# Row loads through six buffers, fewer stores of the indexer parts, and Relu in place in PSUM, in a hybrid attention block

## The chip, the cores and the metric

The kernel runs on one core of one Trainium2 chip. The core has a matrix engine (TensorE, PE in the profile; PEld is its weight load), a vector engine (VectorE, DVE), a scalar engine (ScalarE, ACT), a general engine (GpSimd, POOL) and SyncE (SP), whose queue issues all DMA transfers of this kernel but those of a rare repair path. The metric is the device time of one execution in microseconds (us).

## The reference

One layer over 2048 rows of width 1024, in float32, cut to what matters here:

```python
xn = rms_norm(h, norm_gain[layer])
proj = xn @ w_in[layer]
qa, ka, va, ga, qb, kb, vb, gb, iq, ik, iw, za, zb = jnp.split(proj, offsets, axis=-1)
...
ya = chunked_relpos_attention(qa, ka, va, rel_bias[layer]) * jax.nn.silu(ga)
...
# dsa_sparse_attention, for each block of 128 queries:
logits = jax.nn.relu(jnp.einsum('bqhd,bsd->bqhs', iqb, ik))      # 8 indexer heads of 32
score = jnp.einsum('bqhs,bqh->bqs', logits, iwb).astype(jnp.float32)
_, idx = lax.top_k(score, top_k)                                 # 256 keys per query
...
merged = gate_a * (ya @ w_branch_a[layer]) + gate_b * (yb @ w_branch_b[layer])
h = h + merged @ w_out[layer]
```

The change touches two places: the normalisation of x with the indexer's part of the projection (`iq`, `ik`, `iw`, and `kb`, which rides with them), and the scores (`logits`, `score`).

## The kernel before

**Precision.** PE multiplies a reduced form of float32, so every operand is split: `h` is the value rounded by a copy on ACT, `l` the rest, a subtraction on another engine. A product is three matmuls (`mm3`, L193 to 199): high by high, high by low, low by high.

**The start: indexer projections (L213 to L374).** The rows of x come in four groups of 512, in the order 2, 3, 0, 1. `load_x` (L235) brings a group transposed (k along partitions, eight k-tiles) into one of two tiles `x32`. `squares` (L253) brings the same rows untransposed in four tiles of 128 x 1024 (`xrow`, 512 KB each, tag `gt`, two buffers) and squares and sums them on ACT (L258). `root_columns` (L262) makes the reciprocal roots by Newton steps on DVE. `root_rows` (L269) spreads them on POOL, transposes them on PE (L273) and copies them on ACT (L274). The first two groups are split without the root (`split_u`, L245) and multiplied by it when the product is evacuated. The other two are multiplied first (`split_x`, L207): a multiply on DVE (L209), the copy on ACT (L210), and the subtraction (L211), of eight k-tiles two on DVE and six on POOL. `chain(i, m)` is the product of one group with one of three column tiles m, 24 matmuls of 512 columns in an accumulator; there are five accumulators. `evac_i` (L286) rotates (m = 0), splits into `eh` and `el`, and stores the parts.

The stores go to DRAM: `iqD` (indexer queries) and `kB` (keys of the sparse attention), and to SBUF `ikT` (indexer keys, four copies by partition). Each is a transfer of its own for the high and the low part and for each strip of rows: 16 for m = 0, 2 for m = 1 and 6 for m = 2, so 24 a group.

**The main projections (L1156 to L1182).** `steps` go over column units and groups; each accumulator takes 24 matmuls and is evacuated. After each, `tick` calls `pump(PUMP)`, which lets two generators go on until a budget of cost is used up. The costs are written by hand in the `yield`s.

**The search stage, beside the main projections.** `logits` (L418): for each block of 128 queries, in two halves of four heads and in pieces of up to 512 keys, one matmul per head into a PSUM tile `lg` (five in rotation), Relu on ACT into an SBUF tile `r` (four buffers, L438), and the weighted sum into `sc`: head 0 on DVE (L441), heads 2 and 6 on POOL (L443 and L444), the others on DVE (L446). `search` (L456) finds the threshold of the 256 largest scores of two blocks at a time by eight counting passes, on DVE and ACT, then marks the keys (L514 to L532). `norm_again` (L1146) splits groups 2 and 3 a second time during the main projections; there all subtractions are on POOL.

When both generators have ended and 138 ticks have passed, the attention starts beside the remaining projections (`tick`, L1131), and later runs alone with the branch products, the output product and the final norm.

The order of instructions on each engine and in SyncE's queue comes from the framework's scheduler, which places them by a modelled timeline and by their order in the program. On the chip each engine and each queue runs in that order and waits where an operand or a buffer is not ready.

Of the kernel before, what the change touches and what calls it, by code (L numbers as in the profile page):

```python
# [20 lines left out]
S = 2048  # L21
# [21 lines left out]
PUMP = 3550  # L43
# [8 lines left out]
POOLH = (2, 6)  # L52
# [40 lines left out]
def block_kernel(ctx: ExitStack, tc: tile.TileContext, io, dbg=None):  # L93
# [22 lines left out]
    iqD = scratch("iqD", [2, 32 * H, S])  # L116
    mskD = scratch("mskD", [NT, 128, S], BF16)
# [89 lines left out]
    def split_x(s, k, src, root, e):  # L207

        nc.vector.scalar_tensor_tensor(src, src, gcol[:, k:k + 1], root, op0=OP.mult, op1=OP.mult)  # L209
        nc.scalar.activation(xh[s][:, k], src, AF.Copy)  # L210
        e.tensor_tensor(xl[s][:, k], src, f32(xh[s][:, k]), op=OP.subtract)  # L211

    with ExitStack() as ph:  # L213
# [24 lines left out]
        def load_w(m, k):  # L238
            st = xp.tile([128, 2, 128], F32, name="wis", tag="wis", bufs=4)
# [12 lines left out]

        def squares(i):  # L253
            for j in range(4):
                t = 4 * order[i] + j
                xr = tk.tile([128, D], F32, name="xrow", tag="gt", bufs=2)
                nc.sync.dma_start(xr, x[t * 128:(t + 1) * 128, :])
# [28 lines left out]
        def evac_i(i, m):  # L286
# [17 lines left out]
            e = [xp.tile([128, 512], F32R, name="e" + t, tag="e" + t, bufs=3) for t in "hl"]  # L304
            nc.scalar.activation(e[0], src, AF.Copy)
            (nc.gpsimd if m and i < 2 else nc.vector).tensor_tensor(e[1], src, f32(e[0]), op=OP.subtract)
            for z in range(2):
                q, k_ = iqD[z][:, cols], kB[z][:, cols]
                for dst, r0, r1 in (((q[0:32], 0, 32), (q[192:224], 64, 96), (k_[0:8], 32, 40), (k_[8:16], 96, 104)),
                                    ((q[32:160], 0, 128),),  # L310
                                    ((q[160:192], 0, 32), (q[224:256], 32, 64), (k_[16:64], 64, 112)))[m]:
                    nc.sync.dma_start(dst, f32(e[z][r0:r1]))
                if m == 0:
                    for y in range(2):
                        p = 64 * z + 32 * y
                        nc.sync.dma_start(f32(ikT[p:p + 24, cols]), f32(e[z][40:64]))
                        nc.sync.dma_start(f32(ikT[p + 24:p + 32, cols]), f32(e[z][104:112]))
# [12 lines left out]
        for m in (1, 2):  # L330
            for k in range(0, KT, 2):
                load_w(m, k)
            load_x(0, 4 * m - 4, 4 * m, halves[1])
        split_u(0, halves[0])
        split_u(0, halves[1])
        for k in range(0, KT, 2):
            load_x(1, k, k + 2)
# [986 lines left out]
```

## Time and profile before

| | us |
|---|---|
| median of 3 runs | 2149.0 |
| lowest and highest | 2148.93 and 2151.43 |
| the profiled execution | 2150.69 |
| its span, first to last instruction | 2148.9 |
| first matmul of the main projections, from the span's start | 137.64 |
| last piece of the search (mask store of the last block) issued | 860.8 |

Rows of the profile name an engine, a line of the kernel, the operation, the tile written and the tiles read (`out<-in`), and a count. In the groups of instructions, the busy time in us and the mean in ns of one follow, then the time that the engine stood idle just before them and what ended it (`<-`). In a timeline the first two numbers are the start and the length in us. SPq is SyncE's queue: its rows are DMA issues, not transfers. `xw` and `x` are the two buffers of `x32`, `xa` is an accumulator of the start, `acc` one of the main projections. A busy PE is not PE at its peak, and some matmul records can be missing from a trace.

### The profile page before, as it was taken

The page shows a single profiled execution, that of the slowest core. Times are in us where ns is not written, and L with a number is a line of the kernel's source. Part 1 is how long each engine was busy: PE and PEld are TensorE (multiplying, and loading weights), DVE is VectorE, ACT ScalarE, POOL GpSimd, SP SyncE. Part 2 cuts the span into 40 slices and gives each one's busy share as a digit, 9 for nine tenths or more (in the row PEclk, how much of TensorE's full clock was granted, in tenths as well). Part 3 has the DMA queues.
Part 4 walks back from the last instruction along what each step waited for, and adds up shares of the span by engine and source line. Part 5 has one row for each costly group of instructions (what it writes and reads, how often), then busy time and mean ns, then how long its engine had stood idle before and what let it go on. Part 6 is the DMA issues. An engine that isn't in the chain of part 4 may idle for free.

```text
span 2148.9 us, 33487 instructions
## 1 busy us (share of the span) xinstructions
PE 2038.5 (95%) x10858; PEld 1724.1 (80%) x10858; DVE 1334.1 (62%) x3255; ACT 1200.6 (56%) x2376; POOL 911.5 (42%) x941
## 2 busy tenths in 40 slices
PE   6499999999999999999899999999999999999998
PEld 5377778778886888888797888888889889887786
DVE  3538889696968956001232677866886688875444
ACT  5326555546545554212443787976887688873221
POOL 2426455646346362212321556445444543443420
PEclk9699999999999999999999999999999999999999
DMA  8445343435353332222755966457345641145642
GB/s 288 148 123 182 105 139 129 159 118 198 130 188 135 137 111 103 100 94 96 238 157 185 262 192 205 142 183 237 118 145 173 211 151 61 45 134 185 203 155 88
DMA packets 237939, 330.60 MB, mean 154 GB/s; under 512 B 29888, under 2 KB 120384, under 8 KB 237632
## 3 DMA queue, kind: packets, MB, share of 16 engines
q1 hardware_dynamic: 237760, 328.43, 47.4%
q8 instruction: 86, 1.41, 0.3%
q14 instruction: 93, 0.76, 0.1%
HBM read 221.43 MB, written 105.87 MB: 152 GB/s over the span
## 4 chain that ended last, share of the span: by engine, by line
PE 38%; DMA 6%; ACT 3%; issue 2%; DVE 2%; POOL 2%; SPq 1%; DVEq 0%; ACTq 0%; POOLq 0%
PE d L198 6%; PE po L1221 6%; PE O L969 5%; PE s L944 5%; PE pt L961 4%; PE O L879 3%; PE acc L198 3%; PE pt L869 2%; PE s L834 2%; DMA wst<-wP 1%; DMA mf<-mD 1%; DMA dst<-wB 1%; DVE P L765 1%; DMA dst<-wA 1%; POOL dw L1007 1%
## 5 line engine op out<-in xcount | busy, mean ns | idle before, releaser
L198 PE MATMUL acc<-xh,wt 128*128 128x512 f32 x2304 | 739.7, 395 | 1.3 <-ACT wt L189 1.2
L198 PEld LDWEIGHTS acc<-xh,wt 128*128 128x128 f32 x2304 | 433.1, 188 | 100.6 <-ACT wt L189 1.6
L198 PE MATMUL acc<-xl,wt 128*128 128x512 f32 x1152 | 453.8, 394 | 0.0
L190 POOL TENSOR_TENSOR wt<-wst,wt 128x512 fp32r<-128x512 f32 (+1 forms) x172 | 207.9, 1225 | 350.3 <-ACT wt L189 326.2
L786 POOL TENSOR_TENSOR ptl<-pf,pth 128x512 fp32r<-128x512 f32 (+1 forms) x144 | 179.9, 1249 | 217.0 <-ACT pf L782 157.0
L198 PEld LDWEIGHTS acc<-xl,wt 128*128 128x128 f32 x1152 | 217.3, 189 | 48.9
L789 DVE TENSOR_TENSOR ptl<-pt,pth 128x512 fp32r<-128x512 f32 (+1 forms) x288 | 187.7, 660 | 49.7 <-ACT pth L788 48.6
L446 DVE SCALAR_TENSOR_TENSOR sc<-r,iw,sc 128x512 f32<-128x512 f32 (+2 forms) x190 | 177.0, 951 | 53.5 <-POOL sc L444 35.9
L438 ACT ACTIVATE r<-lg 128x512 f32<-128x512 f32 (+2 forms) x304 | 152.4, 547 | 82.5 <-DVE sc L446 40.1
L944 PE MATMUL s<-kBt,qsB 128*128 128x512 f32 (+3 forms) x640 | 188.7, 385 | 2.5 <-issue 2.2
L788 ACT ACTIVATE pth<-pt 128x512 fp32r<-128x512 f32 (+1 forms) x288 | 161.1, 579 | 27.5 <-PE pt L961 13.2
L961 PE MATMUL pt<-ident,P 128*128 128x128 f32 x1088 | 166.9, 273 | 1.5 <-DVE ptl L789 0.5
L947 ACT ACTIVATE P<-P,mx 128x128 f32<-128x128 f32 (+15 forms) x128 | 154.6, 1208 | 18.5 <-DVE mx L765 17.8
L969 PE MATMUL O<-pth,vBt 128*128 128x256 f32 x544 | 148.2, 290 | 2.1 <-DVE yb L979 1.5
L969 PE MATMUL O<-ptl,vBt 128*128 128x256 f32 x544 | 147.2, 296 | 1.4 <-POOL ptl L786 1.0
L765 DVE CUSTOM_DVE_ANT_0 P<-s,mk,mx 128x512 f32<-128x512 f32 (+2 forms) x192 | 125.1, 652 | 35.2 <-PE s L944 29.3
L189 ACT ACTIVATE wt<-wst 128x512 fp32r<-128x512 f32 (+1 forms) x172 | 92.8, 577 | 87.2 <-DMA wst<-wP 83.6
L961 PEld LDWEIGHTS pt<-ident,P 128*128 128x128 f32 x1088 | 128.4, 140 | 10.5 <-ACT pf L782 1.6
L1007 POOL TENSOR_TENSOR dw<-dst,dw 128x512 fp32r<-128x512 f32 x64 | 82.8, 1293 | 114.0 <-ACT dw L1006 109.6
L494 ACT ACTIVATE jk<-sc,st 128x640 int8<-128x640 f32 (+6 forms) x49 | 71.3, 1455 | 82.3 <-DVE st L512 68.8
L436 PE MATMUL lg<-ikT,iqT 128*128 128x512 f32 (+2 forms) x304 | 98.3, 379 | 18.6 <-ACT r L438 18.6
L944 PEld LDWEIGHTS s<-kBt,qsB 128*128 128x128 f32 x640 | 103.8, 192 | 14.9 <-DVE mx L765 5.2
(233 smaller groups left out, 4234.2 us busy)
## 6 DMA issues: line engine op xcount, KB each, us to landing
wst<-wP SPq DMA_DIRECT2D x132, 256.0 KB
qs<-qA SPq DMA_DIRECT2D x128, 128.0 KB
kk<-kA SPq DMA_DIRECT2D x56, 256.0 KB
vs<-vA SPq DMA_DIRECT2D x56, 256.0 KB
bias<-biasD SPq DMA_DIRECT2D x32, 320.0 KB
xrow<-x SPq DMA_DIRECT2D x16, 512.0 KB
sBD<-ef SPq DMA_DIRECT2D x32, 256.0 KB
sAD<-ef SPq DMA_DIRECT2D x32, 256.0 KB
```

The costliest lines, as they stand in the source:

```text
L190: nc.gpsimd.tensor_tensor(wt[:, 1, k:k + n, c * 128:(c + 1) * 128], st, f32(hi), op=OP.subtract)
L198: nc.tensor.matmul(acc, a, b, start=(i == 0), stop=(i == n - 1))
L438: nc.scalar.activation(r[:, :w], lg[:, :w], AF.Relu)
L446: nc.vector.scalar_tensor_tensor(o_, r[:, :w], wv, o_, op0=OP.mult, op1=OP.add)
L765: nc.vector.tensor_tensor_reduce(dst, ps_, add, 1.0, FMAX if first else mx, OP.add, OP.min, accum_out=mx)
L786: nc.gpsimd.tensor_tensor(lo, pf, f32(hi), op=OP.subtract)
L788: nc.scalar.activation(hi, src, AF.Copy)
L789: nc.vector.tensor_tensor(lo, src, f32(hi), op=OP.subtract)
L944: nc.tensor.matmul(s_ps[:, :w], q[:, h, :], kBt[:, m, a:a + w], start=(m == 0), stop=(m == 1))
L947: nc.scalar.activation(P[:, e, :n], P[:, e, :n], AF.Exp, bias=mx[:, e:e + 1], scale=-1.0, accum_out=st["sum"][:, (u % 2) * 2 + e:(u % 2) * ...
L961: nc.tensor.transpose(pt[:, k, e, :], P[:, e, (kt + k) * 128:(kt + k + 1) * 128], ident)
L969: nc.tensor.matmul(o_, vBt[:, kt + k, :], src[:, k, :], start=(kt + k == 0 and n_ == 0), stop=(kt + k == b and n_ == 1), skip_group_check= ...
```

## The change

In the start:

- `load_rows` takes the row loads out of `squares`. Rows go in turn through three tags of two buffers each: `gt` and `iqT`, which are otherwise used later, and a new `xr`. The loads of group i stand earlier in the program: the first group's ahead of the second group's x, the second's ahead of the main loop, the third's and fourth's inside the first group's turn, with the third group's x between them. The fourth group's x is asked for in the second turn.
- `e` holds both parts in one tile, so one transfer stores both: 6 + 1 + 3 = 10 a group. The indexer keys go to a DRAM scratch `ikD` and from there into `ikT`, four transfers for two groups at a time.
- The subtractions of `evac_i` and `split_x` are all on DVE, those of `norm_again` too.
- The tile that weights pass through (`wis`) gets six buffers for four.

In the search stage:

- Relu writes back into the PSUM tile `lg`, and DVE reads it from there. All eight heads are on DVE; `r` is gone.
- The costs of the `yield`s and the budget `PUMP` (3850 for 3550) are new.

```diff
-PUMP = 3550
+PUMP = 3850
...
-POOLH = (2, 6)
...
+    ikD = scratch("ikD", [2, 32, S])
...
-    def split_x(s, k, src, root, e):
+    def split_x(s, k, src, root):
...
-        e.tensor_tensor(xl[s][:, k], src, f32(xh[s][:, k]), op=OP.subtract)
+        nc.vector.tensor_tensor(xl[s][:, k], src, f32(xh[s][:, k]), op=OP.subtract)
...
-            st = xp.tile([128, 2, 128], F32, name="wis", tag="wis", bufs=4)
+            st = xp.tile([128, 2, 128], F32, name="wis", tag="wis", bufs=6)
...
+        rows_ = {}
+
+        def load_rows(i):
+            for j in range(4):
+                n = rot("rows", 3)
+                t = 4 * order[i] + j
+                rows_[i, j] = (tk, tk, xp)[n].tile([128, D], F32, name="xrow", tag=("gt", "iqT", "xr")[n], bufs=2)
+                nc.sync.dma_start(rows_[i, j], x[t * 128:(t + 1) * 128, :])
+
         def squares(i):
             for j in range(4):
-                t = 4 * order[i] + j
-                xr = tk.tile([128, D], F32, name="xrow", tag="gt", bufs=2)
-                nc.sync.dma_start(xr, x[t * 128:(t + 1) * 128, :])
+                xr = rows_.pop((i, j))
                 nc.scalar.activation(xr, xr, AF.Square, accum_out=ss[:, 4 * i + j:4 * i + j + 1])
...
-            e = [xp.tile([128, 512], F32R, name="e" + t, tag="e" + t, bufs=3) for t in "hl"]
-            nc.scalar.activation(e[0], src, AF.Copy)
-            (nc.gpsimd if m and i < 2 else nc.vector).tensor_tensor(e[1], src, f32(e[0]), op=OP.subtract)
-            for z in range(2):
-                q, k_ = iqD[z][:, cols], kB[z][:, cols]
-                for dst, r0, r1 in (((q[0:32], 0, 32), (q[192:224], 64, 96), (k_[0:8], 32, 40), (k_[8:16], 96, 104)),
-                                    ((q[32:160], 0, 128),),
-                                    ((q[160:192], 0, 32), (q[224:256], 32, 64), (k_[16:64], 64, 112)))[m]:
-                    nc.sync.dma_start(dst, f32(e[z][r0:r1]))
-                if m == 0:
-                    for y in range(2):
-                        p = 64 * z + 32 * y
-                        nc.sync.dma_start(f32(ikT[p:p + 24, cols]), f32(e[z][40:64]))
-                        nc.sync.dma_start(f32(ikT[p + 24:p + 32, cols]), f32(e[z][104:112]))
+            e = xp.tile([128, 2, 512], F32R, name="e", tag="e", bufs=3)
+            nc.scalar.activation(e[:, 0], src, AF.Copy)
+            nc.vector.tensor_tensor(e[:, 1], src, f32(e[:, 0]), op=OP.subtract)
+            q, kb, ik = (t.rearrange("z r n -> r z n")[:, :, cols] for t in (iqD, kB, ikD))
+            for dst, r0, r1 in (((ik[0:24], 40, 64), (ik[24:32], 104, 112), (q[0:32], 0, 32), (q[192:224], 64, 96),
+                                 (kb[0:8], 32, 40), (kb[8:16], 96, 104)),
+                                ((q[32:160], 0, 128),),
+                                ((q[160:192], 0, 32), (q[224:256], 32, 64), (kb[16:64], 64, 112)))[m]:
+                nc.sync.dma_start(dst, f32(e[r0:r1]))
+            if m == 0 and i % 2:
+                half = slice(1024, 2048) if i == 1 else slice(0, 1024)
+                for a in range(4):
+                    nc.sync.dma_start(f32(ikT[32 * a:32 * a + 32, half]), ikD[a // 2][:, half])
...
+        load_rows(0)
+        for k in range(0, KT, 2):
+            load_x(1, k, k + 2)
         split_u(0, halves[0])
         split_u(0, halves[1])
-        for k in range(0, KT, 2):
-            load_x(1, k, k + 2)
         squares(0)
+        load_rows(1)
         for i in range(4):
             for m in range(3):
...
                     squares(1)
+                    load_rows(2)
+                    for k in range(0, KT, 2):
+                        load_x(2, k, k + 2)
+                    load_rows(3)
                 elif m == 0 and i < 3:
                     if i == 1:
                         squares(2)
                         squares(3)
                         root_columns(2, 2)
+                        for k in range(0, KT, 2):
+                            load_x(3, k, k + 2)
                     root_rows(i + 1)
                     for k in range(KT):
-                        split_x(SLOT[order[i + 1]], k, x32[(i + 1) % 2][:, k], roots_[order[i + 1]],
-                                nc.vector if k % 3 == 2 else nc.gpsimd)
+                        split_x(SLOT[order[i + 1]], k, x32[(i + 1) % 2][:, k], roots_[order[i + 1]])
...
-            if i < 2:
-                for k in range(0, KT, 2):
-                    load_x(i + 2, k, k + 2)
...
-                        r = tkl.tile([128, 512], F32, name="r", tag="r", bufs=4)
-                        nc.scalar.activation(r[:, :w], lg[:, :w], AF.Relu)
+                        lg = lg[:, :w]
+                        nc.scalar.activation(lg, lg, AF.Relu)
                         wv = iw[:, b, h:h + 1]
                         if h == 0:
-                            nc.vector.tensor_scalar(o_, r[:, :w], wv, 0.0, op0=OP.mult, op1=OP.add)
-                        elif h in POOLH:
-                            nc.gpsimd.tensor_scalar(r[:, :w], r[:, :w], wv, 0.0, op0=OP.mult, op1=OP.add)
-                            nc.gpsimd.tensor_tensor(o_, o_, r[:, :w], op=OP.add)
+                            nc.vector.tensor_scalar(o_, lg, wv, 0.0, op0=OP.mult, op1=OP.add)
                         else:
-                            nc.vector.scalar_tensor_tensor(o_, r[:, :w], wv, o_, op0=OP.mult, op1=OP.add)
-                        yield 0 if h in POOLH else 230 + w * (0.57 if h == 0 else 1.13)
+                            nc.vector.scalar_tensor_tensor(o_, lg, wv, o_, op0=OP.mult, op1=OP.add)
+                        yield 120 + w * 1.11
...
-            yield 2800
+            yield 3300
...
-                yield n[D] * 1.04 + 300
+                yield n[D] * 1.04 + 220
...
-                yield 2100
+                yield 2700
```

More of the change, by code (lines that the diff above doesn't have):

```diff
@@ L1151, in part @@
             for z in range(2):
-                split_x(SLOT[g], k + z, xs[:, z], roots[g], nc.gpsimd)
+                split_x(SLOT[g], k + z, xs[:, z], roots[g])
         return [lambda k=k: part(k) for k in range(0, KT, 2)]
```

## The prediction

> **What bounds the kernel now.** I read the page first, then busy time by stage, then the waits of TensorE (PE), then the timelines of the stage where PE is idle.
>
> ```profile
> span 2148.9 us, 33487 instructions
> PE 2038.5 (95%) x10858; PEld 1724.1 (80%) x10858; DVE 1334.1 (62%) x3255; ACT 1200.6 (56%) x2376; POOL 911.5 (42%) x941
> ```
> ```profile
> 0.00:38.80 38.80, 31.83 (x192) 29.06 (x192) 14.31 (x29) 19.56 (x41) 10.66 (x109) 1.00 0.92 331
> 38.80:137.60 98.80, 51.43 (x200) 39.66 (x200) 51.37 (x86) 37.35 (x69) 38.12 (x28) 0.74 0.44 136
> 137.60:900.00 762.40, 741.63 (x3356) 604.95 (x3355) 553.33 (x1188) 398.05 (x737) 365.00 (x332) 1.00 0.42 140
> 900.00:1150.00 250.00, 241.33 (x1262) 206.46 (x1261) 46.78 (x131) 83.26 (x205) 65.44 (x67) 0.99 0.45 145
> 1150.00:2149.00 999.00, 972.24 (x5855) 844.00 (x5853) 668.28 (x1822) 662.38 (x1326) 432.25 (x405) 0.99 0.52 162
> ```
>
> The second fence is busy time by stretch: length, then busy us (and instructions) of PE, its weight loads, DVE, ACT and POOL, granted clock, DMA share, GB/s. PE is the bound over the whole, and the change takes no matmul away. So only idle PE and PE at a lower clock can be won: 98.8 - 51.4 = 47.4 us idle in the start (indexer projections, to 137.6), at a mean granted clock of 0.74, and 762.4 - 741.6 = 20.8 us idle in the search stage (to about 900). The 35 us idle after 900 lie in code that the change does not touch.
>
> In the start, these are the waits of PE between 38 and 138 (us in total, times, longest), and the events around the third group:
>
> ```profile
> PE trr L273 <- POOL work L270: 24.8, 3, 17.3
> PE xa L198 <- DVE work L299: 10.4, 1, 10.4
> PE trw L323 <- DVE ea L300: 6.3, 1, 6.3
> PE xa L198 <- DVE xl L211: 5.6, 2, 4.6
> ```
> ```profile
> 42.37 0.17 DVE L264 TENSOR_SCALAR v<-ss 128x4 f32<-128x4 f32 x1 [18.68 <-ACT xrow L258]
> 85.63 1.06 ACT L258 ACTIVATE xrow<-xrow 128x1024 f32<-128x1024 f32 x1 [0.95 <-DMA xrow<-x]
> 86.81 0.17 DVE L264 TENSOR_SCALAR v<-ss 128x8 f32<-128x8 f32 x1 [13.94 <-ACT xrow L258]
> 93.24 1.22 PE L198 MATMUL xa<-xh,w 128*128 128x512 f32 x2 [0.21 <-ACT xh L210]
> 137.64 0.48 PE L198 MATMUL acc<-xh,wt 128*128 128x512 f32 x1
> ```
>
> All four go back to one thing. The roots of a group need the squares of its four row tiles (L258), and the squares wait for the rows' DMA. The third group's first matmul stands at 93.24, 7.6 us after the last square began at 85.63. Why the rows come late is in SyncE's queue:
>
> ```profile
> SPq L257 <- ACT xrow L258: 22.4, 9, 7.5
> ```
> ```profile
> 32.08 24.44 SPq L257 DMA_DIRECT2D xrow<-x  x9
> 59.55 1.84 SPq L312 DMA_DIRECT2D iqD<-eh  x2
> ...
> 73.26 0.43 SPq L312 DMA_DIRECT2D kB<-el  x1
> ...
> 80.82 0.35 SPq L257 DMA_DIRECT2D xrow<-x  x1
> ```
>
> Rows go through two buffers, so each load waits for a square (22.4 us of queue time). Then the 24 stores of the first group's parts hold the queue from 59.55 to 73.69, 14.1 us, and the second group's are mixed with the last row loads, which end at 80.82.
>
> **The start, part by part.** Row loads ahead, through six buffers: no instruction is added, the waits go. What is late next is the DMA rate.
>
> ```profile
> 20.00:30.00 10.00, 10.00 (x64) 9.01 (x63) 3.30 (x4) 4.68 (x9) 1.15 (x2) 1.00 1.04 401
> 0.00:10.00 10.00, 3.25 (x14) 3.20 (x15) 3.99 (x12) 5.75 (x13) 3.93 (x101) 1.00 0.65 198
> 140.00:150.00 10.00, 10.00 (x44) 8.07 (x43) 0.00 (x0) 1.65 (x3) 0.00 (x0) 1.00 0.42 121
> ```
> ```profile
> xrow<-x SPq DMA_DIRECT2D x16, 512.0 KB
> x<-xT SPq DMA_DIRECT2D x8, 512.0 KB
> xw<-xT SPq DMA_DIRECT2D x6, 512.0 KB
> wis<-wI SPq DMA_DIRECT2D x12, 128.0 KB
> xw<-xT SPq DMA_DIRECT2D x4, 256.0 KB
> ```
>
> These five add up to 17,920 KB or 18.35 MB. The first 10 us carry 1.98 MB (198 GB/s), the other 16.4 MB need 40.8 us at 401 GB/s: all has landed at 50.8. The last row lands earlier if it goes ahead of the fourth group's x (2.1 MB, 5.2 us: 45.6), later if tables of 1 MB go ahead of it (53.4). I take 50. Add the 7.6 us from last square to first matmul and 1.4 us for ACT and DVE, which now also evacuate the first two groups around then (before, 10.4 and 6.3 us of PE waits lay there; they go, as the first group's rows are now asked for ahead of the second group's x and its roots, begun at 42.37, come some 20 us earlier): third group at 59 instead of 93.24.
>
> From there to the main projections it took 44.4 us. Two groups of 72 matmuls at 10/44 = 0.227 us are 32.7 us. The subtraction of the split moves from POOL to DVE:
>
> ```profile
> L209 DVE SCALAR_TENSOR_TENSOR x<-x,gcol,work x8: 739/1768/1782, 101.8 to 111.6; 128x512 f32<-128x512 f32 x8
> L211 POOL TENSOR_TENSOR xl<-x,xh x6: 1711/1720/1745, 104.7 to 114.5; 128x512 fp32r<-128x512 f32 x6
> L211 DVE TENSOR_TENSOR xl<-xw,xh x2: 680/1214/1747, 101.2 to 113.3; 128x512 fp32r<-128x512 f32 x2
> ```
>
> The three figures are minimum, median and maximum in ns. With POOL subtracting beside it DVE's L209 takes 1768 at the median and 739 at best, so the two engines slow each other. Alone on DVE a step of the split is 0.74 + 0.68 = 1.42 us. Bounds: 8 steps are 11.4 us at these minima, 28 us at the medians' 3.5 us if the slow rows have another cause; I take the minima, since little is left on POOL there. The third group's first chain is then paced by DVE, 11.4 instead of 24 x 0.227 = 5.4 us, so +6.0; the fourth group's split (11.4) hides under the third's other two chains (10.9) but for 0.5; transposes and evacuation waits 1.3. Sum 32.7 + 6.0 + 0.5 + 1.3 = 40.5, so the main projections begin at 99.5, 38.1 us earlier. I take **37**. Bounds: 47 (row at 45.6, no slack) and 17 (16.6 us of slow split added, and a row 4 us later).
>
> Stores of the parts: 10 a group for 24, and four ikT loads a half from DRAM. An issue took 0.35 (80.82 row) to 0.92 us (59.55 row, two in 1.84): 3.5 to 9.2 us for 14.1. This lies beside PE work now, so I count nothing beyond the above; it costs up to 5 us if stores stand ahead of the last rows. The detour of ikT through DRAM adds a landing. The stores' rows show none of its length; PE's first logits matmul was at
>
> ```profile
> 158.36 1.03 PE L436 MATMUL lg<-ikT,iqT 128*128 128x384 f32 x5
> ```
>
> so 20.7 us of main projections cover it. Six weight buffers for four: nothing counted.
>
> **The search stage.** Relu in place, heads read from PSUM, no head on POOL.
>
> ```profile
> L446 DVE SCALAR_TENSOR_TENSOR sc<-r,iw,sc 128x512 f32<-128x512 f32 (+2 forms) x190 | 177.0, 951 | 53.5 <-POOL sc L444 35.9 <-ACT r L438 14.2
> L441 DVE TENSOR_SCALAR sc<-r,iw 128x512 f32<-128x512 f32 (+2 forms) x38 | 26.4, 694 | 36.8 <-ACT r L438 36.6 <-DMA iqT<-iqD 0.2
> L438 ACT ACTIVATE r<-lg 128x512 f32<-128x512 f32 (+2 forms) x304 | 152.4, 547 | 82.5 <-DVE sc L446 40.1 <-PE lg L436 19.5 <-POOL sc L444 14.6
> L674 DVE SCALAR_TENSOR_TENSOR el<-acc,eh 128x512 fp32r<-128x512 f32 x30 | 20.6, 686 | 21.9 <-ACT eh L673 20.8 <-DMA qB<-el 0.8 <-issue 0.3
> PE lg L436 <- ACT r L438: 18.6, 18, 2.8
> L446 DVE SCALAR_TENSOR_TENSOR sc<-r,iw,sc 128x512 f32<-128x512 f32 x125 | 127.2, 1034 | 30.9 <-POOL sc L444 20.8 <-ACT r L438 8.0
> ```
>
> DVE spends 177.0 + 26.4 = 203.4 us on six heads of eight and waits 35.9 more for POOL's sum. The same operation with one input in PSUM (L674) takes 686 ns at 512 columns, where L446 takes 1034. Scaled by that ratio, 304 heads cost 304 x 0.951 x 686/1034 = 192 us. Bounds: at L446's own 0.951 they cost 289 (86 more), at half of L674's 96 (107 less). I take 192, the nearest row being the same operation from PSUM to SBUF. So DVE does all eight heads in 11 us less than six. The later splits add 16 subtractions (16 x 0.68 = 10.9) and make the multiply beside them shorter. DVE's 553 us of 762 stay about 550: not the bound. Relu into PSUM has no row; L438's 547 ns and twice that are the ends, and ACT at 398 of 762 us covers even the second.
>
> Against it stands depth. A logits tile was free for PE once ACT had read it, with four more buffers of r behind; now it is free once DVE has read it, in order behind the search's long operations: five in flight for nine. PE's own waits there were 18.6 us in 18 places. Bounds: all 18.6 go; or each of the 18 gets longer by four heads of 0.69 us, +50. DVE's time per head, waits for POOL included, falls by a fifth ((203.4 + 35.9) to 192), and the new costs in the yields (120 + 1.11w, which at 512 gives 688, for L674's 686) spread heads better over the projections. I take **-6**. The thread costs add up to 510.9 thousand at 3850 a tick, 132.7 ticks, against 452.6 at 3550, 127.5; attention opens after tick 138 either way.
>
> [...]
>
> **Sum.** The profiled execution took 2150.7 us (span 2148.9 and 1.8 around it), 1.7 above the median of 2149.0. 2150.7 - 37 - 6 = **2108 us**, about 2.0% off. I call 0.2%, some 4 us, no change.
>
> **The rivals.**
> 1. *Start half won.* Stores of the first group's parts stand ahead of the last rows in SyncE's queue, or DVE does all sixteen L209 before the first subtraction, as it did eight before 101.2. The third group then starts near 75, gain 20: 2150.7 - 20 - 2 = 2129. For it: the queue did just that (73.26 and 80.82 rows). Chance 0.15.
> 2. *Better.* Row ahead of the last x, and PE's logits waits gone: -47 - 12 = 2092. Chance 0.11.
> 3. *Slower: the logits tiles.* PE stands at L436 for a tile that DVE has not read. It decides when the added wait passes the 37 us won in the start: 0.12 us for each of 304 heads. At the bound above, 18 waits longer by 2.8 us, it adds 50: 2150.7 - 37 + 50 = 2164. For it: five tiles, and one in-order DVE at 553/762 = 73%. Against: DVE gets less to do per head. Chance 0.08.
> 4. *PSUM heads dear.* If a head from PSUM costs DVE what L446 costs (0.951 us), DVE gets 86 us more than before in a stage with 209 idle. PE saw 18.6 us of the 203.4 us of heads before, 9%: 8 us, and the -6 is gone. 2150.7 - 37 + 8 = 2122. Chance 0.04. [...]
> 5. *It does not do what it says.* Squares still gate the loads (ACT is in order, and buffer seven waits for square one), so the rows land as late: 2149. Chance 0.04.
>
> **How the numbers follow.** Forecast (2097 to 2122) 0.58, rivals 0.15, 0.11, 0.08, 0.04, 0.04. The range 2090 to 2136 leaves out rivals 3 and 5 and the ends of 1 and 2. Faster: 0.58 + 0.15 + 0.11 + 0.04 = 0.88; same 0.04; slower 0.08.
>
> **What would show it.** Right: last row square before 55, third group's first matmul near 59, main projections near 100, clock near 1.0 in between; no SPq wait of L257 over some us; L446 near 690 ns; PE's lg waits under 18.6, now released by DVE. Wrong: squares past 70; L209 still near 1200 ns without POOL beside it; PE idle at L436 over 40 us.

## The result and the profile after

The changed kernel takes 2097.96 us (median of 4 runs, 2091.42 to 2099.17) against 2149.36 us of the kernel before on the same chip: a ratio of 0.9753, with a 95% interval of 0.9731 to 0.9774. That is 51 us less. 2108 was forecast, with a range of 2090 to 2136. The profiled execution took 2098.9 us.

Busy time by stretch follows, for the kernel after (columns as in the prediction). The stretches are counted from the first matmul of the main projections, at 108.23 us: the start ahead of it, its first 50 us, the next 150, the next 400, and what follows 858.23. The 150 us between the last two are left out; they hold 649 matmuls in both kernels.

```profile
38.80:108.23 69.43, 47.97 (x197) 37.79 (x197) 46.35 (x89) 30.10 (x60) 17.19 (x13) 0.83 0.57 200
108.23:158.23 50.00, 45.73 (x195) 37.22 (x194) 21.67 (x57) 23.38 (x52) 10.45 (x8) 0.93 0.64 207
158.23:308.23 150.00, 150.00 (x660) 122.37 (x659) 104.63 (x323) 81.85 (x165) 37.93 (x39) 1.00 0.38 127
308.23:708.23 400.00, 400.00 (x1909) 335.27 (x1909) 321.76 (x720) 225.03 (x410) 90.21 (x91) 1.00 0.45 153
858.23:2097.10 1238.87, 1202.45 (x7063) 1041.64 (x7061) 717.57 (x1952) 741.24 (x1524) 493.98 (x469) 0.99 0.51 159
```

The same stretches of the kernel before, counted from its first main matmul at 137.64:

```profile
137.64:187.64 50.00, 48.66 (x217) 39.27 (x216) 20.02 (x23) 21.91 (x49) 23.05 (x22) 1.00 0.64 201
187.64:337.64 150.00, 142.70 (x621) 114.65 (x620) 129.39 (x356) 85.34 (x173) 74.92 (x76) 1.00 0.39 129
337.64:737.64 400.00, 387.88 (x1820) 319.42 (x1819) 324.01 (x638) 217.69 (x399) 205.30 (x187) 0.99 0.44 149
887.64:2148.90 1261.26, 1225.93 (x7168) 1060.46 (x7166) 715.06 (x1952) 747.54 (x1533) 499.95 (x474) 0.99 0.50 158
```

Read the matmul counts, not only the busy time: in equal time they say how far PE has come. In the first 50 us of the main projections the changed kernel is 22 matmuls *behind* (195 for 217), in the next 150 us 39 ahead, in the next 400 us 89 ahead. Together that is 106, and at 0.2095 us each (400 / 1909) 22 us. The other 29.4 us are the earlier beginning of the main projections (137.64 to 108.23). 29.4 + 22 is nearly the whole difference of the spans, 51.8. After that nothing is won: PE is idle for 36.4 us of the last stretch, for 35.3 before. In the middle stretches before, PE was idle for 7.3 and 12.1 us and also a little slower while busy (0.2131 us a matmul for 0.2095 in the 400 us); after, it is never idle there.

The start in the timeline of the kernel after (start, length, then the instruction; PE, ACT, DVE and SyncE's queue SPq put together in order of time):

```profile
42.96 1.06 ACT L265 ACTIVATE xrow<-xrow 128x1024 f32<-128x1024 f32 x1 [1.25 <-DMA xrow<-x]
46.29 0.56 SPq L300 DMA_DIRECT2D cs<-csI  x1
46.95 0.54 SPq L260 DMA_DIRECT2D xrow<-x  x1
...
52.60 0.20 ACT L330 ACTIVATE iw<-trw 128x32 f32<-128x32 f32 x1 [2.71 <-PE trw L329]
52.70 1.05 ACT L265 ACTIVATE xrow<-xrow 128x1024 f32<-128x1024 f32 x1
...
57.89 1.04 ACT L265 ACTIVATE xrow<-xrow 128x1024 f32<-128x1024 f32 x1
60.10 0.17 DVE L271 TENSOR_SCALAR v<-ss 128x8 f32<-128x8 f32 x1
...
67.23 5.39 DVE L209 SCALAR_TENSOR_TENSOR xw<-xw,gcol,work 128x512 f32<-128x512 f32 x8 [2.61 <-ACT work L281]
68.70 1.65 PE L198 MATMUL xa<-xh,w 128*128 128x512 f32 x3 [0.22 <-ACT xh L210]
...
108.23 0.48 PE L198 MATMUL acc<-xh,wt 128*128 128x512 f32 x1
```

The last row load is issued at 46.95 and the third group's first matmul stands at 68.70, 21.8 us later. Between 44.0 and 52.7 ACT does no square: in its order copies stand ahead, those of the first group's evacuation and the small one of the indexer weights (L330), which waits 2.71 us for PE's transposes. Then six squares run back to back to 58.9. That does not make ACT the only limit. In this kernel the row loads whose landing the trace has took 6.3 to 10.6 us from issue to landing, which puts the last row at 53.3 to 57.6. Where the same load's landing is on record, in the kernel with the roots apart (below), it was issued at 46.90 and landed 9.7 us later, at 56.6 (the view of L260 from 46 to 48 us):

```profile
DMA to landing us min/median/max: 9.7/9.7/9.7
```

By that estimate the last square, begun at 57.89, came some 1.3 us after its row. The roots' small steps on DVE begin at 60.10 and end at 64.6; they stand between instructions of 0.7 us that evacuate the second group. All eight multiplies (L209) come before the first subtraction, 5.4 us during which PE has only the high parts.

PE's waits from 38 to 108 us, then those for logits tiles over the search stage:

```profile
PE xa L198 <- DVE work L306: 8.3, 1, 8.3
PE trw L329 <- DVE rs2y L134: 6.6, 1, 6.6
PE trr L280 <- POOL work L277: 4.1, 2, 3.3
PE xa L198 <- DVE xl L211: 2.9, 1, 2.9
...
PE lg L446 <- DVE sc L453: 3.8, 1, 3.8
PE lg L446 <- DMA ikT<-ikD: 0.5, 1, 0.5
```

Set beside the four waits that the prediction lists for the start: 24.8 us for the roots' rows (trr) became 4.1, and 5.6 for the low parts (xl) became 2.9. The other two stayed: 10.4 us for the evacuation (work) became 8.3, and 6.3 ahead of the weights' transposes (trw) became 6.6. 18.6 us of waits for logits tiles in 18 places became 4.3 in two. Groups of instructions of the kernel after:

```profile
L453 DVE SCALAR_TENSOR_TENSOR sc<-lg,iw,sc 128x512 f32<-128x512 f32 x175 | 129.8, 746 | 50.8 <-ACT lg L448 45.5
L448 ACT ACTIVATE lg<-lg 128x512 f32<-128x512 f32 x200 | 109.8, 577 | 39.1 <-PE lg L446 38.1
L209 DVE SCALAR_TENSOR_TENSOR x<-x,gcol,work 128x512 f32<-128x512 f32 x8 | 5.5, 739 | 0.0
```

A head of 512 columns takes 746 ns for 1034, and DVE now waits for ACT, not for GpSimd.

### The profile page after: what moved, and what is told of

The parts are those of the page before. It is cut to its first block, busy times and chain, and to the rows that moved or that the text cites. A ratio compares the mean times of both kernels' runs of the same rounds, so it can differ in the third digit from the quotient of the medians.

```text
span 2097.1 us, 33111 instructions
## 1 busy us (share of the span) xinstructions
PE 2027.5 (97%) x10858; PEld 1724.6 (82%) x10858; DVE 1309.3 (62%) x3363; ACT 1200.8 (57%) x2376; POOL 696.4 (33%) x757
## 4 chain that ended last, share of the span: by engine, by line
PE 41%; DMA 5%; ACT 2%; DVE 2%; issue 2%; SPq 1%; POOL 1%; DVEq 0%; ACTq 0%; POOLq 0%
PE po L1228 8%; PE d L198 8%; PE O L976 5%; PE s L951 5%; PE pt L968 5%; PE O L886 3%; PE acc L198 2%; PE s L841 2%; PE pt L876 2%; DMA vA<-eht 1%; DMA wst<-wP 1%; DMA dst<-wB 1%; DVE P L772 1%; DMA qs<-qA 1%; DMA dst<-wA 1%
## 5 line engine op out<-in xcount | busy, mean ns | idle before, releaser
L190 POOL TENSOR_TENSOR wt<-wst,wt 128x512 fp32r<-128x512 f32 (+1 forms) x172 | 206.2, 1215 | 604.5 <-ACT wt L189 590.0
L453 DVE SCALAR_TENSOR_TENSOR sc<-lg,iw,sc 128x512 f32<-128x512 f32 (+2 forms) x266 | 178.9, 680 | 90.4 <-ACT lg L448 82.2
L448 ACT ACTIVATE lg<-lg 128x512 f32<-128x512 f32 (+2 forms) x304 | 150.5, 525 | 53.9 <-PE lg L446 53.0
L846 ACT ACTIVATE P<-P,mx 128x640 f32<-128x640 f32 (+4 forms) x128 | 98.0, 767 | 23.7 <-DVE mx L772 23.2
L976 PEld LDWEIGHTS O<-pth,vBt 128*128 128x128 f32 x544 | 102.8, 189 | 10.5 <-ACT pth L795 2.5
```

What stands on the lines that cost most here:

```text
L190: nc.gpsimd.tensor_tensor(wt[:, 1, k:k + n, c * 128:(c + 1) * 128], st, f32(hi), op=OP.subtract)
L448: nc.scalar.activation(lg, lg, AF.Relu)
L453: nc.vector.scalar_tensor_tensor(o_, lg, wv, o_, op0=OP.mult, op1=OP.add)
L976: nc.tensor.matmul(o_, vBt[:, kt + k, :], src[:, k, :], start=(kt + k == 0 and n_ == 0), stop=(kt + k == b and n_ == 1), skip_group_check= ...
```

## The experiments

They ran in three groups on three chips; each ratio is against the kernel before on the same chip (medians 2150.73, 2149.25 and 2153.61 us). All kernels compute the whole layer.

**The start alone.** The kernel after, with the search stage, its costs and `norm_again` of before.

```diff
-PUMP = 3850
+PUMP = 3550
+POOLH = (2, 6)
...
-                        lg = lg[:, :w]
-                        nc.scalar.activation(lg, lg, AF.Relu)
+                        r = tkl.tile([128, 512], F32, name="r", tag="r", bufs=4)
+                        nc.scalar.activation(r[:, :w], lg[:, :w], AF.Relu)
...
+                        elif h in POOLH:
+                            nc.gpsimd.tensor_scalar(r[:, :w], r[:, :w], wv, 0.0, op0=OP.mult, op1=OP.add)
+                            nc.gpsimd.tensor_tensor(o_, o_, r[:, :w], op=OP.add)
...
```

> The kernel after with the search stage of before put back (Relu into r, heads 2 and 6 on GpSimd, the old costs and budget, the second splits' subtractions on GpSimd). After, the main projections began at 108.2 us for 137.6 before. Theory: the two halves of the change add up, so the start alone gives its 29.4 us: 2149.4 - 29 = 2120, main projections at 108 to 110, PE's wait for logits tiles still near 18.6 us. Rival: the earlier start is given back in the search stage, which was filled with DVE work: 2130 to 2145, logits waits over 25 us.

Measured: 2117.33 us, ratio 0.9849 (0.9829 to 0.9868), 33.4 us less. Main projections at 109.66. The logits waits are there nearly as before (14.8 us for 18.6), and in the first 50 us of the main projections this kernel does 202 matmuls, also fewer than the 217 of the kernel before:

```profile
PE lg L447 <- ACT r L449: 14.8, 17, 2.8
```
```profile
109.66:159.66 50.00, 45.80 (x202) 36.29 (x201) 25.00 (x61) 24.76 (x57) 21.47 (x20) 1.00 0.65 207
```

**The search alone.** The kernel before, with the search stage and the costs of after.

```diff
...
-POOLH = (2, 6)
...
-                        nc.scalar.activation(r[:, :w], lg[:, :w], AF.Relu)
+                        lg = lg[:, :w]
+                        nc.scalar.activation(lg, lg, AF.Relu)
...
-                        yield 0 if h in POOLH else 230 + w * (0.57 if h == 0 else 1.13)
+                        yield 120 + w * 1.11
...
```

> The kernel before with the search stage of after (Relu in place in PSUM, all heads on DVE, the new costs and budget); the start, and the second splits' subtractions on GpSimd, as before. Theory: the search part alone gives some 22 us (16 us of idle PE and 6 us of slower PE): 2127, PE's wait for logits tiles under 5 us, main projections still at 137.6. Rival: part of it came from the second splits on DVE or from the earlier start: 2133 to 2140, logits waits of 8 to 15 us.

Measured: 2124.56 us, ratio 0.9885 (0.9862 to 0.9908), 26.2 us less. Its waits for logits tiles, and its first 50 us from the first main matmul at 137.40 (in the next 150 and 400 us PE is never idle, with 660 and 1910 matmuls):

```profile
PE lg L435 <- DVE sc L440: 0.4, 1, 0.4
```
```profile
137.40:187.40 50.00, 48.37 (x217) 39.32 (x215) 16.96 (x30) 21.38 (x48) 11.76 (x10) 1.00 0.64 201
```

The two halves add to 59.6 us, together they give some 53 (2.47% of 2150.73). The intervals leave room for plain addition. In the first 50 us this kernel does 217 matmuls like the kernel before, the changed kernel 195; those 22 are about 5 us (50 / 217 = 0.23 us each). They do not show that the halves disturb each other: the start alone is 15 behind as well, so most of this loss comes with the new start and is already in its 33.4 us. The roots experiment below looks at what PE waits for there.

**Row loads alone.** The kernel before with `load_rows`, its six buffers and the new order of the loads; 24 stores and the split on GpSimd stay.

```diff
...
-                xr = tk.tile([128, D], F32, name="xrow", tag="gt", bufs=2)
-                nc.sync.dma_start(xr, x[t * 128:(t + 1) * 128, :])
+                xr = rows_.pop((i, j))
...
+        load_rows(0)
+        for k in range(0, KT, 2):
+            load_x(1, k, k + 2)
...
```

> The kernel before with only the row loads through six buffers and the new order of the loads of x; 24 stores a group, splits on GpSimd and search as before. Theory: the rows are most of the start's gain; without the other edits the third group's split is slowed by GpSimd beside it, so main projections at 112 to 118 and 2124 to 2130. Rival: the 24 stores hold SyncE's queue ahead of the last row loads, so the last square stands past 65 (58 after) and main projections at 122 or later, 2134 or more.

Measured: 2132.21 us, ratio 0.9919 (0.9900 to 0.9939), main projections at 120.40, last square at 56.07. The main projections begin later than the 112 to 118 that were expected. So the rows alone give 17 of the start's 29 us: they are early, but the split on two engines is slow, as its multiply shows (1500 ns at the mean here, 739 in the kernel after), and the 24 stores hold the start back too, as a run below shows for the kernel after (5 to 7 us):

```profile
L209 DVE SCALAR_TENSOR_TENSOR x<-x,gcol,work 128x512 f32<-128x512 f32 x8 | 11.5, 1500 | 0.0
```

**Two row buffers.** The kernel after, with all rows through `gt`'s two buffers.

```diff
-                n = rot("rows", 3)
+                n = rot("rows", 1)
```

> The kernel after with the rows through the two buffers of gt alone, the new order of loads kept. Theory: the six buffers let the rows come at the DMA's rate; with two, each load waits for a square, and the loads of x behind it in the queue wait too: third group at 75 to 85 for 68.7, main projections at 114 to 124, 2104 to 2114. Rival: the order of the loads and the fewer stores did it: third group at 68 to 72, time within 3 of after.

Measured: 2114.31 us, ratio 0.9820 (0.9804 to 0.9836); third group at 83.83, main projections at 123.31. SyncE's queue waits for squares again:

```profile
SPq L260 <- ACT xrow L265: 17.8, 10, 6.0
```

Against the kernel after beside it (2099.5) that is 14.8 us: six buffers are worth about that, and 13 us show in the start (123.31 for 110.19).

**24 stores a group.** The kernel after, with the stores of before (one a part and strip, `ikT` filled directly).

```diff
...
-                nc.sync.dma_start(dst, f32(e[r0:r1]))
+                    nc.sync.dma_start(dst, f32(e[z][r0:r1]))
+                if m == 0:
+                    for y in range(2):
+                        p = 64 * z + 32 * y
+                        nc.sync.dma_start(f32(ikT[p:p + 24, cols]), f32(e[z][40:64]))
...
```

> The kernel after with the 24 stores a group of before (two tiles e, ikT written from SBUF) put back. Rows alone had the main projections at 120.4 us, all start edits at 108.2 to 109.7. Theory: the stores issue beside PE work and come after the last row loads, so they are worth little: main projections at 108 to 112, time within 4 us of after. Rival: their 14 us of queue hold back the tables and the weights of the main projections, so they are most of the 11 us: main projections at 116 or later, 2105 or more.

Measured: 2102.09 us, ratio 0.9777 (0.9754 to 0.9800); third group at 73.14, main projections at 115.30. PE waits 8.6 us for the roots' rows where the kernel after waits 4.1:

```profile
PE trr L279 <- POOL work L276: 8.6, 2, 7.8
```

The start is 5 to 7 us later, past the 108 to 112 that were expected, but the intervals of the whole times overlap: a loss in the total is not shown.

**The split on GpSimd again.** The kernel after, with six of eight subtractions of the start's split on GpSimd.

```diff
...
-        nc.vector.tensor_tensor(xl[s][:, k], src, f32(xh[s][:, k]), op=OP.subtract)
+        e.tensor_tensor(xl[s][:, k], src, f32(xh[s][:, k]), op=OP.subtract)
...
+                                nc.vector if k % 3 == 2 else nc.gpsimd)
```

> The kernel after with six of eight subtractions of the start's third and fourth splits on GpSimd again (the second splits stay on DVE). Theory: GpSimd beside DVE slows both, L209 at 1250 to 1770 ns for 740, and this is most of the 11 us that rows alone lack: main projections at 115 to 119, time some 8 us above after. Rival: the split is off PE's path either way: main projections at 108 to 111, time that of after.

Measured: 2102.52 us, ratio 0.9788 (0.9765 to 0.9810); main projections at 113.67. The multiply by itself, with minimum, median and maximum in ns:

```profile
L209 DVE SCALAR_TENSOR_TENSOR xs<-xs,gcol,roots x16: 744/750/753, 132.1 to 619.1; 128x512 f32<-128x512 f32 x16
L209 DVE SCALAR_TENSOR_TENSOR x<-x,gcol,work x8: 740/1773/1785, 77.7 to 87.5; 128x512 f32<-128x512 f32 x8
```

In one kernel, the same operation takes 750 ns at the median where GpSimd has no part in the split and 1773 where it subtracts six k-tiles of eight. That settles why L209 was slow before (1768 at the median). The main projections begin 3.5 to 5.4 us later than in the two profiles of the kernel after (110.19 and 108.23), less than was expected (115 to 119). In the whole time a loss is not clear: the interval overlaps that of the first measurement of the kernel after (up to 0.9774), but not that of the second, below (up to 0.9763).

Rows (17.2 us), split (3.5 to 5.4) and stores (5 to 7) together come to 26 to 30 us, about the 29.4 of the start. The evacuation's subtractions on DVE and the six weight buffers were not tried by themselves.

**Relu into SBUF, no head on GpSimd.** The kernel after with the tile `r` again, four buffers; all heads on DVE.

```diff
-                        lg = lg[:, :w]
-                        nc.scalar.activation(lg, lg, AF.Relu)
+                        r = tkl.tile([128, 512], F32, name="r", tag="r", bufs=4)
+                        nc.scalar.activation(r[:, :w], lg[:, :w], AF.Relu)
+                        lg = r[:, :w]
```

> The kernel after with Relu into the four SBUF buffers r again; all eight heads on DVE, now from SBUF. Theory A: DVE's heads got cheaper because GpSimd no longer reads SBUF beside them; then a head of 512 takes some 740 ns here as well, PE's wait for logits tiles stays under 5 us, and the time is that of after, 2098 within 3. Theory B: the source in PSUM is what makes the head cheap; then a head of 512 takes 900 to 1030 ns, and the time is 2104 to 2115.

Measured: 2094.95 us, ratio 0.9753 (0.9726 to 0.9780), the same as the kernel after. So Relu in place is worth nothing that can be measured; that GpSimd takes no heads is what counts. The heads in three kernels (this one, the kernel after, and the start alone with two heads on GpSimd; minimum, median, maximum in ns):

```profile
L454 DVE SCALAR_TENSOR_TENSOR sc<-r,iw,sc x266: 465/746/1832, 117.9 to 779.5; 128x512 f32<-128x512 f32 x85, 128x384 f32<-128x384 f32 x24, 128x256 f32<-128x256 f32 x24
```
```profile
L453 DVE SCALAR_TENSOR_TENSOR sc<-lg,iw,sc x266: 457/742/754, 116.3 to 781.1; 128x512 f32<-128x512 f32 x84, 128x384 f32<-128x384 f32 x25, 128x256 f32<-128x256 f32 x24
```
```profile
L457 DVE SCALAR_TENSOR_TENSOR sc<-r,iw,sc x190: 471/748/1860, 117.6 to 775.0; 128x512 f32<-128x512 f32 x125, 128x384 f32<-128x384 f32 x35, 128x256 f32<-128x256 f32 x30
```

The medians agree; what differs is the tail. From PSUM no head takes more than 754 ns. From SBUF some take 1832, in this kernel few (mean 830 at 512 columns), with heads on GpSimd many (1025 in the start alone). This is the pattern of L209. Two heads of 512 columns show it, each begun while GpSimd subtracts for the weights' split (L190): the first of this kernel, the second of the kernel after.

```profile
735.32 1.30 POOL L190 TENSOR_TENSOR wt<-wst,wt 128x512 fp32r<-128x512 f32 x1
735.55 1.62 DVE L454 SCALAR_TENSOR_TENSOR sc<-r,iw,sc 128x512 f32<-128x512 f32 x1 [3.97 <-ACT r L448]
```
```profile
737.88 1.30 POOL L190 TENSOR_TENSOR wt<-wst,wt 128x512 fp32r<-128x512 f32 x1
738.37 0.75 DVE L453 SCALAR_TENSOR_TENSOR sc<-lg,iw,sc 128x512 f32<-128x512 f32 x1 [0.75 <-ACT lg L448]
```

With both inputs in SBUF the head ends at 737.17, 0.55 us after the subtraction's end at 736.62. Counted in the trace, all 28 heads over 1 us in this kernel end so, 0.54 to 0.55 us after such a subtraction at 512 columns (17 of them), 0.41 at 384 and 0.28 at 256. So the end of a slow head goes by the end of the subtraction, not by the head's own start. In the kernel after, 57 of the 266 heads run beside a subtraction on GpSimd and none is longer for it (754 ns at most). The head above is lengthened by less than GpSimd's whole 1.30 us (1.62 us for 0.75); 0.23 us of the subtraction had gone by when it began. Why the place of the input matters is not shown.

**The costs of before.** The kernel after, with the yields and the budget of before.

```diff
-PUMP = 3850
+PUMP = 3550
...
-                        yield 120 + w * 1.11
+                        yield 0 if h in (2, 6) else 230 + w * (0.57 if h == 0 else 1.13)
...
```

> The kernel after with the yields and the budget of before (3550 a tick, heads 2 and 6 at no cost). Theory: the cheaper heads did it, the costs only spread the work: PE's logits waits 4 to 10 us, time within 5 us of after. Rival: the new costs are what frees PE: waits of 15 us or more, 2108 or more.

Measured: 2095.87 us, ratio 0.9752 (0.9725 to 0.9779): the same. The costs are worth nothing that can be measured.

**Three logits tiles for five.** A test of the rival that the tiles run out.

```diff
-                        ln = rot("lg", 5)
+                        ln = rot("lg", 3)
```

> The kernel after with the logits in three PSUM tiles in rotation for five. Theory of the prediction's third rival: a tile is free only once DVE has read it, so fewer tiles let PE wait for DVE: 15 to 40 us of PE waits at the logits for 4.3, 2108 to 2130. Other theory: DVE has so much slack that three do: waits under 10, 2098 to 2104.

Measured: 2101.19 us, ratio 0.9759 (0.9743 to 0.9774), beside 2099.5 us of the kernel after on that chip, with overlapping intervals. The waits grow little:

```profile
PE lg L446 <- DVE sc L453: 3.8, 3, 3.4
```

Even three tiles are enough. Depth is not what bounds this stage.

**The roots apart.** The third group's roots waited in the kernel after for the squares of the fourth, since both are made in one pass over 8 columns (L271). Here each group has its own.

```diff
                         squares(2)
-                        squares(3)
-                        root_columns(2, 2)
+                        root_columns(2, 1)
...
+                    else:
+                        squares(3)
+                        root_columns(3, 1)
```

> The kernel after with the roots of the third and fourth group made apart (four Newton columns each), so that the third group does not wait for the fourth group's squares, which move behind the third group's first product in the program. After, the last six squares ran back to back from 52.7 to 58.8 though their rows had been asked for by 47, and the third group's first matmul came at 68.7. Theory: ACT's order, not the DMA, is what is late now, so the third group starts 4 to 8 us earlier, main projections at 101 to 105, time 2090 to 2094. Rival: the evacuation of the second group on DVE and PE's first two products end about then anyway: third group at 66 or later and the time of after.

Measured: 2091.2 us, ratio 0.9734 (0.9709 to 0.9759); the interval overlaps that of the kernel after (0.9731 to 0.9774), so a gain over it is not shown by this run. The third group begins 6.4 us earlier than in the kernel after, but the main projections at 109.23, no earlier:

```profile
62.27 1.22 PE L198 MATMUL xa<-xh,w 128*128 128x512 f32 x2 [2.40 <-ACT xh L210]
68.26 0.79 PE L198 MATMUL xa<-xh,w 128*128 128x512 f32 x1 [4.76 <-DVE work L306]
```

The expected earlier start did not come: much of the time won turned into a wait for the second group's evacuation. Nor was ACT's order the only thing late, as the theory had it: the last row landed at 56.6 here too. Yet the first 50 us of the main projections changed:

```profile
109.23:159.23 50.00, 50.00 (x226) 41.08 (x224) 23.60 (x66) 26.33 (x58) 10.20 (x8) 1.00 0.66 204
```

That is 31 matmuls more than the 195 of the kernel after, some 7 us (24 more than the 202 of its second profile, below). The order on DVE differs. First the kernel after (DVE and PE), then this one (DVE):

```profile
116.30 2.78 DVE L453 SCALAR_TENSOR_TENSOR sc<-lg,iw,sc 128x384 f32<-128x384 f32 x4
130.34 1.42 DVE L209 SCALAR_TENSOR_TENSOR xs<-xs,gcol,roots 128x512 f32<-128x512 f32 x2 [11.25 <-DMA wst<-wP]
131.67 0.61 DVE L453 SCALAR_TENSOR_TENSOR sc<-lg,iw,sc 128x384 f32<-128x384 f32 x1
...
132.33 0.69 PE L446 MATMUL lg<-ikT,iqT 128*128 128x384 f32 x1 [3.77 <-DVE sc L453]
```
```profile
124.79 0.62 DVE L455 SCALAR_TENSOR_TENSOR sc<-lg,iw,sc 128x384 f32<-128x384 f32 x1 [2.09 <-ACT lg L450]
129.58 1.42 DVE L209 SCALAR_TENSOR_TENSOR xs<-xs,gcol,roots 128x512 f32<-128x512 f32 x2 [4.18 <-DMA xs<-xT]
```

In the kernel after, the multiply of `norm_again` stands in DVE's order behind five heads (L451 and these four L453) and waits 11.25 us for a transfer: its operand is `xs`, though the profile names `wst` as the last to come. The heads behind it hold the logits tiles, and PE stands 3.77 us at L446. In this kernel six heads go ahead of the multiply, the sixth at 124.79, its tile is free in time, and PE has no wait for a logits tile in these 50 us. The granted clock is 1.00 there for 0.93. So the traces explain the wait by the order on DVE, and the wait with the lower clock makes up the difference in matmuls; no run changes this order alone. What else held the main projections at 109 us was not taken apart.

**The kernel after again, and the roots apart with later transposes.** Five rounds each on one chip; in the second, also the weights' transposes `weights_t` come one turn later.

```diff
...
-                    else:
-                        weights_t(i - 1)
+                    elif i > 1:
+                        weights_t(i - 2)
...
+        weights_t(2)
         weights_t(3)
```

> The kernel after once more, as it is, as the measure for the runs beside it: 2098 within 4. Its first profile had the main projections at 108.2 us.

> The kernel after with the roots of the third and fourth group made apart, and the transposes of the indexer weights (whose copy held ACT up until 53) one turn later. With the roots apart alone the third group started at 62.3 for 68.7, yet PE stood 12.6 us for L306, the evacuation of the first two groups, and the main projections began no earlier (109.2). Theory: without the copy ahead of them the squares end at 53 to 55, the third group starts at 57 to 60, and main projections at 103 to 106, 3 to 5 us under after in the same runs. Rival: the evacuations on DVE set the start, so main projections at 108 or later and the time of after within 2.

Measured: 2099.5 us, ratio 0.9750 (0.9737 to 0.9763), for the kernel after; 2092.7 us, ratio 0.9714 (0.9701 to 0.9727), for the other. These intervals do not overlap: it beats both kernels. Its third group begins at 62.11, not at 57 to 60, and its first main matmul stands at 109.86 for 110.19, so the expected gain in the start did not come here either. The first 50 us of main projections, the kernel after first:

```profile
110.19:160.19 50.00, 46.51 (x202) 37.40 (x201) 23.58 (x61) 24.14 (x55) 10.25 (x8) 0.97 0.66 205
```
```profile
109.86:159.86 50.00, 48.34 (x216) 39.08 (x215) 22.02 (x57) 24.57 (x54) 10.21 (x8) 1.00 0.64 205
```

14 matmuls more, some 3 us, and 0.3 us in the start; the profiled spans differ by 4.8 (2097.7 and 2092.9), the medians by 6.8. The rest of the gain has no place in these rows and stays open.

## Why the prediction was right, and where it was off

**Direction and mechanism held.** The rows were the limit of the start (two buffers put the main projections back by 13 us), and most of PE's waits for logits tiles went. 51 us came for 43. The sum came out near because its two parts missed in opposite ways, the start by 8 us too much and the search by 16 too little; part of the number is luck.

**Start: 29.4 us for 37.** The step that was mis-sized is "third group at 59". It stands at 68.70, and the rest of the start came as forecast: from there to the main projections 39.5 us (68.70 to 108.23) for 40.5, with L209 and L211 alone at 739 and 675 ns, the minima that were taken. Of the three terms of the 59, the landing taken at 50 was the largest miss: the last row was issued only at 46.95 and landed at some 56.6, by the estimate above. A second table of 512 KB (cs, 46.29) was asked for just ahead of it, as in the prediction's case for 53.4; where the rest of the delay comes from was not taken apart. The 1.4 us for ACT and DVE were about right, some 1.3 from landing to square. The 7.6 us from last square to first matmul became 10.8 (57.89 to 68.70), with the roots' steps on DVE standing between 2.7 us of the second group's evacuation. In all 6.6 - 0.1 + 3.2 = 9.7 us.

The 10.4 and 6.3 us of waits that the sum held to be gone are there as 8.3 and 6.6. The first ends with the first group's evacuation, which DVE begins at 44.12, behind the second group's roots; these still waited for a row (the square at 42.96). The second ends with the second group's evacuation, for which DVE waits 2.84 us for GpSimd (the table cs). And the wait for the low parts depends on the split: 2.9 us, and 4.6 with GpSimd in it. So not all four waits "go back to one thing", the rows. After the roots were made apart the third group came at 62.27 and the main projections at 109.23; PE's waits for the evacuation (L306) then came to 12.6 us, 4.76 of them at 68.26.

Of the signs named ahead, hardly a wait of the row loads for a square (0.6 us in all), and few waits for logits tiles, 3.8 of the 4.3 us released by DVE, came as said. Missed were the last square before 55 (57.89), the main projections near 100 (108.23), the clock near 1.0 in the start (0.83 from 38.80 to 108.23), and heads near 690 ns (746).

**The parts of the start.** "Stores counted at nothing, up to 5 us": with 24 stores the start is 5 to 7 us later, though no loss of time is shown. "The split on DVE": 3.5 to 5.4 us of the start. Six buffers: 13 us. Rival 1, the stores ahead of the last rows, did not occur: the last row was issued at 46.95, the first store at 48.35. Its other mechanism, all L209 first, did occur for the eight of the third group (67.23 to 72.6), and PE waited 2.9 us for the first low part.

**Search: 22 us for 6.** This is the largest miss. The bound "all 18.6 go" was nearly what happened, since depth did not matter (three tiles are enough) and the waits had come from GpSimd's heads: DVE waited 35.9 us for GpSimd's sum, and its own heads were slowed beside GpSimd (1034 ns at 512 columns, 746 after). The forecast took a third of the bound although its own sum had DVE's time per head fall by a fifth. It also priced the heads by a row that reads PSUM; with Relu into SBUF the median is the same, so it is GpSimd's absence that makes them cheap. On top, PE was slower while busy in the stretches with waits (0.2131 for 0.2095 us a matmul), some 6 us in the 400 us, which no term of the sum had. In the first 50 us some 5 us are given back; in the trace of the kernel after, PE's longest wait there is for heads that stand on DVE behind a transfer of `norm_again`.

**Heads.** 192 us were forecast for eight heads; 178.9 us for seven (L453) and some 26 for head 0 (25 at 743 ns and 13 shorter ones) make about 205. The 0.686 of L674 was 8% low; L209's 739 would have been the better row. The 10.9 us of later splits came as forecast (16 at 682 ns).

**Rival 3, the tiles**, falls: with three tiles the median is 1.7 us longer, well within the intervals. Its mechanism shows once, for 3.8 us, and behind a transfer instead of a search operation. **Rival 4, heads dear from PSUM**, falls too. At the median a head takes 742 ns from PSUM and 746 from SBUF, so for this operation, which reads its other tensor from SBUF, the measurement decides against it. **Rival 5** falls: in the kernel after, the row loads (L260) wait 0.6 us for squares in all, where with two buffers they wait 17.8 us.

**Costs of the yields**, expected to spread heads better: nothing measurable.

## What to carry to other kernels

Where two engines share a sum or slow each other, look at the spread of an operation's times, not its mean: here 740 at best and 1773 at the median was the sign that another engine was in the way, and DVE did eight heads alone in about the time of six beside GpSimd (some 205 us for 203.4). Take the landing of a load, not its issue, as the time when work can begin: here they lay some 10 us apart. Loads ahead of time through more buffers paid here only up to the next in-order queue (last row at some 56.6 us, the third group's first matmul at 68.70), so list what stands in front of the newly ready work on ACT and DVE. An instruction that waits for a transfer should not stand in an engine's order ahead of work that frees buffers for the bound engine: here DVE waited 11.25 us at such a place, and PE 3.77 us for what stood behind it.

## What was not expected of the hardware

- A head of 512 columns on VectorE with both inputs in SBUF, some 750 ns where nothing slowed it, took up to 1832 ns beside a GpSimd subtraction of two SBUF tiles. Each of the 17 over 1 us ended 0.55 us after such a subtraction. With one input in PSUM all 266 heads stayed within 754 ns, 57 of them beside such a subtraction.
- ScalarE's Relu of 512 columns took 577 ns back into PSUM and 602 into SBUF.
- Head 0, a scaling with a single tensor input, was the other way round: 741 ns at the median from PSUM, 478 from SBUF (38 heads each, 25 of them of 512 columns).
- In the 400 us of the kernel before in which PE waited 12.1 us, its matmuls between the waits were slower too: 0.2131 us at a granted clock of 0.99, against 0.2095 at 1.00 in the kernel after, where it never waited.
